# Opening of a fused matmul, GELU, matmul: four x tiles loaded and transposed in halves of K, and the first products in another order

## The chip, the cores and the metric

The kernel runs on one core of a Trainium2 chip. The metric is the time of one execution on the device in microseconds (us); of several executions the median counts. The core has a matrix engine (TensorE, PE in the profile; its weight loads are PEld), a vector engine (VectorE, DVE), an activation engine (ScalarE, ACT), a general engine (GpSimd, POOL), and a queue engine (SyncE, SP). DMAs are issued from SP, ACT and POOL; those that POOL issues also convert float32 in memory to bfloat16 on the core.

## What is computed

```python
batch, m, k, h, n = 16, 512, 768, 3072, 768
y = np.matmul(x, w1) + b1                    # x (16, 512, 768), w1 (768, 3072)
y = 0.5 * y * (1.0 + erf(y / np.sqrt(2.0)))
return np.matmul(y, w2).astype(np.float32)   # w2 (3072, 768)
```

All tensors are float32. The 16 x 512 rows of x are one list of 8192 rows.

## The kernel before, in words

Rows are worked on in passes (`pairs`) of 768 rows, that is two halves of 384, or six tiles of 128 rows; ten such passes, and one of 512 rows. In a pass the kernel first makes `g = gelu(x w1 + b1)`, transposed, with the hidden dimension on the partitions, then `g w2`. Both products use block schemes with fewer multiplications (seven products P1 to P7 for the first, fifteen M0 to M14 for the second); sums and differences of blocks are formed on VectorE. The forms of w1 are stored to a scratch tensor in memory (`w1f`) and read again in later passes; those of w2 stay on the core.

The first pass can't begin like the others, as nothing is loaded. Its opening is written out by hand, and the order of the calls is the order on each engine:

- x tiles 0 and 1 come as float32 through SP (`xw`, lines 466 and 467) and are converted by VectorE and ScalarE; tiles 2 to 5 come through POOL with conversion (`load_x0`, line 451) into `xb0`.
- w1 comes in groups of 384 columns (`load_w1`, line 351), each with six slices of 128 rows of K (`KC` = 6, `KH` = 3). Group 0 is loaded slice by slice (slices 0 and 1 together), group 1 in two halves, the others whole. Groups 2 and 3 lie in the tile `xft`.
- `turn_x0` (line 456) transposes a tile on TensorE: six transposes of 128 x 128 into a PSUM bank (two banks, `turns`, in turn), then a copy on VectorE into `xt`. Half 0 of `xt` holds tiles 0 to 2, half 1 tiles 3 to 5.
- `busy(n)` (line 440) issues n matmuls of 512 columns on zeros, whose result nobody reads: fillers.
- `first(half, c0, c1, k0, k1)` (line 498) multiplies w1 slices k0 to k1 of group 0 with columns c0 to c1 of a half of `xt`, for three blocks of 128 hidden columns at once; after the last slice and column, the GELU follows on ScalarE (`gelu1`).
- The bias is loaded as 24 rows, transposed on TensorE (line 529) into a corner of the second transpose bank, and copied to `b1t` by ScalarE.

Then `plain` (line 424) multiplies w1 groups 1, 2 and 3 with all of `xt`; `sum_x` and `form_w1` form sums on VectorE (copies for some w1 forms on ScalarE); and `step0` begins the seven-product scheme with block 3 (`product1`, line 148): P1 goes into a PSUM bank, ScalarE copies it to a second one (`c11`), and P2 adds into that.

Two things set the order around the change. Each engine takes its instructions in program order, and each waits for semaphores of those it depends on. And loads issued on POOL use eight semaphores in turn, so POOL issues a load only when the eighth one before it has landed.

## Time and profile before

| What | us |
|---|---|
| median of three runs | 873.79 (873.76 to 875.26) |
| profiled execution, its time | 873.71 |
| its span, first to last instruction | 871.9 |
| TensorE busy in the span | 866.8 (99%) |
| VectorE busy | 598.3 (69%) |
| ScalarE busy | 400.5 (46%) |
| first product (`first`) begins | 7.41 |
| first `plain` product begins | 15.34 |
| DMA bytes moved | 145.94 MB, mean 167 GB/s |

Times in the profile count from the start of the span. A line of a timeline has start, length, engine, source line, operation, output and inputs, shape and count; in brackets stands the idle time of the engine before it and what ended that. A line of the chain has start, length, and engine, tile and line. Matmuls are pipelined: one of 128 columns lasts 0.22 us but the next starts 0.056 us later. The length of a group of matmuls so holds one tail of about 0.16 us.

### The profile page before, as it was taken

The numbers are of one execution on the slowest core, as the hardware profiler recorded it, in microseconds if no ns is written. First come the engines' busy times: TensorE is split into PE (matmuls) and PEld (weight loads), VectorE is DVE, ScalarE is ACT, GpSimd is POOL, SyncE is SP. The second block draws the span as 40 slices with busy tenths as digits, with TensorE's granted clock in tenths as the row PEclk, the third lists the DMA queues.
The fourth block names the chain that finished last, engine by engine and source line by source line (L and its number), as shares of the span: only waits on it lengthen the run. The fifth ranks groups of instructions, "written<-read, shape, count | busy, mean of one in ns | idle before, by whom it ended". The sixth has DMA issues, their size and how long they took to land.

```text
span 871.9 us, 14069 instructions
## 1 busy us (share of the span) xinstructions
PE 866.8 (99%) x5479; PEld 531.2 (61%) x5479; DVE 598.3 (69%) x1090; ACT 400.5 (46%) x798; POOL 87.4 (10%) x160
## 2 busy tenths in 40 slices
PE   9999999999999999999999999999999999999998
PEld 5666556666666666666666666666666666666775
DVE  5799869657765775676577657756765776577654
ACT  3741673167127514731671275147316712751560
POOL 6120111010110001000101100010001011000000
PEclk9999999999999999999999999999999999999999
DMA  9997588176627736671756277366717663761521
GB/s 193 207 239 223 200 317 167 60 230 202 149 70 243 198 89 177 200 180 61 231 197 152 80 234 206 80 179 199 177 63 229 200 151 79 235 195 55 191 87 73
DMA packets 88935, 145.94 MB, mean 167 GB/s; under 512 B 50828, under 2 KB 68388, under 8 KB 88868
## 3 DMA queue, kind: packets, MB, share of 16 engines
q1 hardware_dynamic: 64256, 93.60, 35.7%
q0 software_dynamic: 24432, 50.73, 24.1%
q8 instruction: 43, 0.70, 0.3%
q10 hardware_dynamic: 180, 0.70, 0.2%
q14 instruction: 24, 0.20, 0.1%
HBM read 121.81 MB, written 33.42 MB: 178 GB/s over the span
## 4 chain that ended last, share of the span: by engine, by line
PE 97%; DMA 2%; POOL 0%; ACT 0%; DVE 0%; issue 0%; DVEq 0%; ACTq 0%; POOLq 0%
PE ps L237 47%; PE ps L162 45%; PE ps L431 3%; PE ps L822 1%; DMA w1f<-ot 1%; DMA st<-in_x_dram 1%; PE ps L504 0%; POOL w1t L78 0%; ACT g L145 0%; ACT ot L103 0%; POOL st L78 0%; DVE ps L113 0%; ACT ps L103 0%; DVE ev L113 0%; PE ps L459 0%
## 5 line engine op out<-in xcount | busy, mean ns | idle before, releaser
L162 PEld LDWEIGHTS <-w1t 128*128 128x128 bf16 x2421 | 236.9, 98 | 144.7 <-issue 1.4
L237 PE MATMUL ps<-w2t,g 128*128 128x384 bf16 x1512 | 257.8, 326 | 0.0
L162 PE MATMUL ps<-xft,w1t 128*128 128x384 bf16 (+1 forms) x1368 | 255.3, 320 | 0.3 <-ACT ps L103 0.3
L145 ACT ACTIVATE g<-ps,b1t 128x384 bf16<-128x384 f32 (+1 forms) x404 | 218.6, 570 | 74.5 <-PE ps L162 58.7
L237 PEld LDWEIGHTS <-g 128*128 128x128 bf16 x1512 | 147.9, 98 | 97.3
L162 PE MATMUL ps<-xt,w1t 128*128 128x384 bf16 (+1 forms) x1035 | 200.8, 320 | 0.1
L110 DVE TENSOR_TENSOR ot<-ot,ps 128x384 f32<-128x384 f32 x231 | 125.5, 552 | 106.0 <-PE ps L237 51.4
L237 PE MATMUL ps<-w2t,st 128*128 128x384 bf16 x1008 | 170.7, 326 | 0.0
L103 ACT COPY ot<-ps 128x384 f32<-128x384 f32 x129 | 60.8, 478 | 225.1 <-PE ps L237 206.3
L237 PEld LDWEIGHTS <-st 128*128 128x128 bf16 x1008 | 98.6, 98 | 65.2
L103 ACT COPY ps<-ps 128x384 f32<-128x384 f32 (+1 forms) x124 | 56.3, 454 | 142.5 <-PE ps L162 142.5
L113 DVE TENSOR_TENSOR ev<-ps,ev 128x384 f32<-128x384 f32 (+1 forms) x120 | 65.4, 545 | 73.5 <-PE ps L162 73.3
L113 DVE TENSOR_TENSOR ps<-ps,ev 128x384 f32<-128x384 f32 (+1 forms) x120 | 66.3, 553 | 44.0 <-PE ps L162 41.8
L105 DVE COPY ev<-ps 128x384 f32<-128x384 f32 (+1 forms) x120 | 65.0, 542 | 21.8 <-PE ps L162 21.7
L145 ACT ACTIVATE g<-ev,b1t 128x384 bf16<-128x384 f32 (+1 forms) x120 | 72.7, 606 | 15.3 <-DVE ev L113 15.3
L113 DVE TENSOR_TENSOR st<-g 128x1024 bf16<-128x1024 bf16 x107 | 73.0, 683 | 0.9 <-ACT g L145 0.9
L78 POOL DMA_DIRECT2D out_dram<-ot x60 | 32.7, 546 | 340.9 <-DVE ot L110 337.6
L113 DVE TENSOR_TENSOR g<-g 128x1024 bf16<-128x1024 bf16 x84 | 57.5, 684 | 0.5
L78 POOL DMA_DIRECT2D xb<-in_x_dram x38 | 20.5, 543 | 310.8 <-DMA xt<-xb 309.1
L110 DVE TENSOR_TENSOR g<-g 128x1024 bf16<-128x1024 bf16 x42 | 29.0, 690 | 1.1
L110 DVE TENSOR_TENSOR st<-st,g 128x1024 bf16<-128x1024 bf16 x42 | 28.9, 688 | 0.7
L431 PE MATMUL ps<-xt,w1t 128*128 128x384 bf16 x132 | 22.4, 326 | 0.0
(87 smaller groups left out, 291.6 us busy)
## 6 DMA issues: line engine op xcount, KB each, us to landing
w1t<-w1f SPq DMA_DIRECT2D x113, 672.0 KB, 5.2
out_dram<-ot POOLq DMA_DIRECT2D x60, 384.0 KB, 2.6
xb<-in_x_dram POOLq DMA_DIRECT2D x38, 192.0 KB, 4.7
w2t<-in_w_dram POOLq DMA_DIRECT2D x8, 576.0 KB, 20.4
w1f<-ot POOLq DMA_DIRECT2D x6, 672.0 KB, 8.2
ot<-in_x_dram POOLq DMA_DIRECT2D x18, 192.0 KB, 7.2
w1t<-in_w_dram POOLq DMA_DIRECT2D x4, 576.0 KB, 20.1
w1f<-ev SPq DMA_DIRECT2D x2, 672.0 KB, 3.5
```

What stands on the lines that cost most here:

```text
L78: inorder(queue.dma_start(out=out, in_=in_))
L103: inorder(nc.scalar.copy(out=dst, in_=src))
L105: inorder(nc.vector.tensor_copy(out=dst, in_=src))
L110: inorder(nc.vector.tensor_tensor(out=dst, in0=a, in1=b, op=ALU.add))
L113: inorder(nc.vector.tensor_tensor(out=dst, in0=a, in1=b, op=ALU.subtract))
L145: inorder(nc.scalar.activation(out=g[:, place_h(hc), half, :w], in_=src, func=ACTF.Gelu, bias=b1t[:, hc:hc + 1], scale=sign))
L162: inorder(nc.tensor.matmul(out=ps[:, :w], lhsT=forms[:, kc, :], rhs=moving1(m, kc, w, xs), start=(kc == 0 and m in ("P1", "P7")), stop=(kc ...
L237: inorder(nc.tensor.matmul(out=ps[:, :NB], lhsT=lhs[:, c, :], rhs=w2t[:, c, WF[m], :], start=(m in OPENS and c == 0), stop=(c == QC - 1), ...
L431: inorder(nc.tensor.matmul(out=py[:, :HW], lhsT=lhs[:, kc, (j % 3) * P:(j % 3 + 1) * P], rhs=xt[:, kc, half, :], start=(kc == 0), stop=(kc ...
L822: inorder(nc.tensor.matmul(out=ps[:, :c1 - c0], lhsT=lhs[:, c, :], rhs=w2t[:, c, WF[f], c0:c1], start=(f == terms[0][0] and c == 0), stop= ...
```

## The change

All of it is in the opening. Line numbers shift by up to 16 behind it: `first` has its products at line 511 and `turn_x0` its transposes at line 463.

- Tiles 2 to 5 are loaded in two halves of K each (columns 0 to 383 and 384 to 767), eight loads instead of four. The first halves stand beside w1 slices 0 to 2, the second halves among and behind slices 3 to 5. Slices 3 and 4 come in one load instead of two.
- `turn_x0` transposes a range of K: three transposes and a copy of 384 columns a call for tiles 2 to 5. The two banks are used in turn by the order of the calls, not by the tile.
- The calls of `first` are cut and ordered anew, to follow the order of the loads.
- `busy` takes a width. Seven fillers of 512 columns stay; five of 128 follow them; two of 512 and two of 128 stand where five of 512 stood.
- The bias transpose moves from before tile 0 to between tiles 0 and 1, and the bias copy on ScalarE so behind the conversion of tile 1.

```diff
-    def busy(n):
+    def busy(n, w=4 * P):
         for _ in range(n):
-            inorder(nc.tensor.matmul(out=pw[:], lhsT=warm[:, 0:P], rhs=warm, start=True, stop=True))
+            inorder(nc.tensor.matmul(out=pw[:, :w], lhsT=warm[:, 0:P], rhs=warm[:, :w], start=True, stop=True))
...
-    def load_x0(n):
-        dma(nc.gpsimd, out=xb0[:, n, :], in_=xf[n * P:(n + 1) * P, :])
+    def load_x0(n, k0, k1):
+        dma(nc.gpsimd, out=xb0[:, n, k0 * P:k1 * P], in_=xf[n * P:(n + 1) * P, k0 * P:k1 * P])
 
     turns = (bank(), bank())
 
-    def turn_x0(n, engine):
-        pt = turns[n % 2][:, :KC * P // 2].bitcast(BF16).rearrange("p (kc c) -> p kc c", kc=KC)
-        for kc in range(KC):
+    turned = 0
+
+    def turn_x0(n, k0=0, k1=KC):
+        nonlocal turned
+        pt = turns[turned % 2][:, :KC * P // 2].bitcast(BF16).rearrange("p (kc c) -> p kc c", kc=KC)
+        turned += 1
+        for kc in range(k0, k1):
             inorder(nc.tensor.transpose(out=pt[:, kc, :], in_=xb0[:, n, kc * P:(kc + 1) * P], identity=ident))
         half, c0 = place(HW, n)
-        copy(engine, xt[:, :, half, c0:c0 + P], pt)
+        copy("dve", xt[:, k0:k1, half, c0:c0 + P], pt[:, k0:k1])
...
-    load_x0(2)
+    load_x0(2, 0, KH)
     load_w1(0, 0, 2)
...
-    load_x0(3)
+    load_x0(3, 0, KH)
     load_w1(0, 2, 3)
-    load_w1(0, 3, 4)
-    load_x0(4)
-    load_w1(0, 4, 5)
-    load_x0(5)
+    load_x0(4, 0, KH)
+    load_x0(5, 0, KH)
+    load_x0(2, KH, KC)
+    load_w1(0, 3, 5)
+    load_x0(3, KH, KC)
     load_w1(0, 5, 6)
+    load_x0(4, KH, KC)
+    load_x0(5, KH, KC)
     load_w1(1, 0, KH)
     load_w1(1, KH, KC)
...
     busy(7)
+    busy(5, P)
+    copy("dve", xb0[:, 0, :], xw[:, 0, :])
+    turn_x0(0)
+    copy("act", xb0[:, 1, :], xw[:, 1, :])
+    busy(1)
     tb = turns[1][:, 448:448 + HC]
     inorder(nc.tensor.transpose(out=tb, in_=b1s, identity=ident32[:HC, :HC]))
     copy("act", b1t[:, :HC], tb)
-    copy("dve", xb0[:, 0, :], xw[:, 0, :])
-    turn_x0(0, "dve")
-    copy("act", xb0[:, 1, :], xw[:, 1, :])
-    busy(2)
-    turn_x0(1, "dve")
     busy(1)
-    turn_x0(2, "dve")
-    busy(2)
+    turn_x0(1)
+    turn_x0(2, 0, KH)
+    busy(2, P)
     first(0, 0, 2 * P, 0, 2)
+    turn_x0(3, 0, KH)
     first(0, 2 * P, HW, 0, 2)
-    turn_x0(3, "dve")
-    first(0, 0, HW, 2, 3)
-    first(1, 0, P, 0, 3)
+    first(0, 0, 2 * P, 2, 3)
+    first(1, 0, P, 0, 1)
+    turn_x0(4, 0, KH)
+    first(1, 0, P, 1, 2)
+    first(0, 2 * P, HW, 2, 3)
+    turn_x0(5, 0, KH)
+    first(1, 0, P, 2, 3)
+    first(1, P, 2 * P, 0, 1)
+    turn_x0(2, KH, KC)
+    first(1, P, 2 * P, 1, 2)
+    first(1, 2 * P, HW, 0, 2)
+    first(1, P, HW, 2, 3)
     first(0, 0, HW, 3, 4)
-    first(1, 0, P, 3, 4)
-    turn_x0(4, "dve")
+    turn_x0(3, KH, KC)
     first(0, 0, HW, 4, 5)
-    first(1, 0, P, 4, 5)
-    first(1, P, 2 * P, 0, 3)
-    turn_x0(5, "dve")
-    first(1, P, 2 * P, 3, 5)
+    first(1, 0, P, 3, 5)
+    turn_x0(4, KH, KC)
     first(0, 0, HW, 5, 6)
+    turn_x0(5, KH, KC)
     first(1, 0, P, 5, 6)
-    first(1, P, 2 * P, 5, 6)
-    first(1, 2 * P, HW, 0, 6)
+    first(1, P, 2 * P, 3, 6)
+    first(1, 2 * P, HW, 3, 6)
```

## The prediction, made before the result was known

> **What bounds the kernel now.** I read the page from the top: span, busy times, then the chain of work that ended last.
>
> ```profile
> span 871.9 us, 14069 instructions
> PE 866.8 (99%) x5479; PEld 531.2 (61%) x5479; DVE 598.3 (69%) x1090; ACT 400.5 (46%) x798; POOL 87.4 (10%) x160
> ...
> PE 97%; DMA 2%; POOL 0%; ACT 0%; DVE 0%; issue 0%; DVEq 0%; ACTq 0%; POOLq 0%
> ```
>
> TensorE carries 97% of the chain. Work on another engine is worth only the holes that it leaves in PE, and the change touches only the first 15 us. So I read the same chain for the first 60 us.
>
> ```profile
> 5.43 5.66 DMA st<-in_x_dram
> 11.09 0.05 issue
> 11.14 0.51 PE ps L459 x6
> 11.65 0.03 issue
> 11.68 1.33 PE ps L504 x15
> 13.01 0.34 PE ps L459 x6
> 13.34 2.16 PE ps L504 x33
> 15.50 8.78 PE ps L431 x54
> ```
>
> Until 11.09 the chain hangs on a landing (x tile 4); from 11.68 on it is PE without a hole. Next the timeline of the opening, for its order and its prices.
>
> ```profile
> 1.19 3.17 PE L442 MATMUL ps<-st 128*128 128x512 bf16 x7 [1.19 <-DVE st L471]
> ...
> 5.19 0.83 ACT L103 CAST st<-ot 128x768 bf16<-128x768 f32 x1 [0.39 <-DMA ot<-in_x_dram]
> ...
> 6.08 0.51 PE L459 MATMUL ps<-st 128*128 128x128 bf16 x6 [0.28 <-ACT st L103]
> ...
> 6.70 1.03 DVE L105 COPY xt<-ps 128x768 bf16<-128x768 bf16 x2 [0.74 <-PE ps L459]
> ...
> 6.97 0.59 PE L442 MATMUL ps<-st 128*128 128x512 bf16 x2
> ...
> 7.41 1.15 PE L504 MATMUL ps<-xt,w1t 128*128 128x256 bf16 x12
> ...
> 15.34 6.01 PE L431 MATMUL ps<-xt,w1t 128*128 128x384 bf16 x36
> ```
>
> Products begin at 7.41, and the next stage (L431) starts at 15.34. Prices, from starts: 56 ns for a product or transpose of 128 columns (0.34 for six), 109 for 256 columns, 162.5 for 384 (36 in 5.85 plus a tail of 0.16). Last, ScalarE behind the opening, which will matter:
>
> ```profile
> 22.00 0.83 ACT L103 COPY w1t<-xft 128x768 bf16<-128x768 bf16 x1
> 22.74 0.58 ACT L145 ACTIVATE g<-ps,b1t 128x384 bf16<-128x384 f32 x1
> 23.21 0.82 ACT L103 COPY ev<-xft 128x768 bf16<-128x768 bf16 x1
> 23.93 1.05 ACT L145 ACTIVATE g<-ps,b1t 128x384 bf16<-128x384 f32 x2
> 24.87 0.49 ACT L103 COPY ps<-ps 128x384 f32<-128x384 f32 x1
> ```
>
> From 22.00 ACT works without a hole; it started there because w1 group 3 (in xft) landed at 21.90 (issue 10.43, 11.5 to landing).
>
> **The change, part by part.**
>
> *The holes in the products.* From 7.41 to 15.34 are 7.93 us. The 78 products before are 60 x 0.056 + 6 x 0.109 + 12 x 0.1625 = 5.96, the transposes of tiles 3 to 5 18 x 0.056 = 1.01. The rest, 0.96, is holes, all before 11.68: waits for x tiles, w1 pieces and one DVE copy. After, there are again 78 products: 57 x 0.056 + 12 x 0.109 + 9 x 0.1625 = 5.96. Behind the first product stand 21 transposes (the second half of tile 2 moves behind it): 1.18, so 0.17 more.
>
> *Are the halves there in time?* Landings are from the list of DMA issues, asked load by load: issue plus time to landing. One unit is 96 KB: a half tile or one w1 slice. Before, tile 2 landed at 6.06 and w1 slice 5, twelve units later, at 13.04: 0.58 a unit. The next 18 units, to 21.90, took 0.49 each. A half tile has the shape of a w1 slice (128 rows of 384): slices landed 0.50 to 0.54 apart where the stream ran freely, whole tiles 0.91 to 1.15. So six halves cost 3.0 to 3.2 against 3.01 for tiles 3 to 5. For four tiles that is 0 to +0.3; I take +0.1, since both rows hold the same bytes. The first half of tile 2 lands at about 5.6 (half a tile earlier). Counting units at 0.49 to 0.58, against when PE gets there: w1 slices 3 and 4 at 10.0 to 10.8 against 11.1; second half of tile 3 at 10.5 to 11.4 against 11.6; of tile 4 at 11.5 to 12.6 against 12.7; of tile 5 at 12.0 to 13.1 against 13.4; the earlier ones have 0.4 or more. All hold, the slow end barely.
>
> *POOL.* Four more x loads at 0.55 and one w1 load fewer (0.56). POOL may have eight loads out: at 8.66 before, it sat 0.34 until an x tile had landed. Now this wait comes three loads earlier, in front of the second half of tile 3. POOL gets there at about 7.0, and the load it waits for lands at 5.6; the following ones have 0.7 or more. Behind it queue the w1 groups: group 1 is issued near 9.25 instead of 7.52, but the queue ahead is full until about 12.6. Nothing, then; without that cover the 1.7 us would show at 15.
>
> *DVE.* Four copies of 768 columns become eight of 384, each about 0.36 (0.56 less the 0.20 that 384 columns take at their share). A half turn's data are usable 0.78 after its first transpose (0.33 transposing, 0.04, 0.36, 0.05). One place in the new order is shorter: between the transposes of tile 3's second half (0.17) and its products stands only 0.49 of other products; PE waits 0.12. DVE's next work, the x sums, starts near 13.9 as before (13.85).
>
> *The bias and the fillers.* The bias transpose moves behind tile 0. It writes into the same PSUM bank as tile 1's transposes, so these gain a wait for ACT's bias copy, which now stands behind the 0.83 cast ending at 6.02. Its 0.18 overlaps the cast's tail: 0 to 0.18, I take 0.14, as successive ACT rows start about 0.09 before the former ends. Behind that wait stand tile 1 and every product. Tile 1 starts at 6.22, its DVE copy 0.62 later (6.08 to 6.70 before) takes 0.56, and the first product starts at 7.45 instead of 7.41: 0.04 lost. The fillers that go (five of 512 become two of 512 and two of 128 from here on) gain nothing, since the copy sets the start; the five of 128 before tile 0 fill a wait for its cast.
>
> *Sum for the opening:* 0.96 - 0.17 - 0.12 - 0.04 = 0.63 earlier: L431 at 14.71. Its w1 halves landed at 14.50 and 16.00, needed at 14.71 and 16.17.
>
> *What is late next.* The ACT rows. Product P2 adds into a bank that ACT fills by the copy of 24.87 to 25.36, so it can't begin before 25.43, unless group 3 lands earlier; before, PE got there at 26.07. Cap: 0.64 less the delay of group 3. With my +0.1 the gain is 0.54. Behind it nothing caps again: the w2 chunks landed 1.3 or more before DVE took them (chunk 7: 56.06 against 57.40), and the PE hole of 0.48 at 114.84 hangs on a store that POOL issues after an activation, so it moves along.
>
> The profiled execution took 873.71 us around its span of 871.9; the median of the runs is 873.79, 0.08 above. 873.79 - 0.54 = **873.25**, 0.06% faster. A change under 0.2% (1.75 us) is about what this kernel's measurement can't tell from none.
>
> **The rivals.**
>
> *The halves run freer.* At 0.49 a unit from the start, group 3 lands up to 1 us earlier and the cap goes; without the bias wait the opening gives 0.77 to 0.9. 872.95. For it: 0.49 later in the same trace. Against: 0.58 in this very stretch.
>
> *No gain.* One DMA engine lagged: slice 3 landed 1.29 after slice 2, where 0.5 is usual. Such a lag on a second half stops PE for 0.3 to 0.6, since only 0.2 to 0.3 of cover is left at the slow end; or group 3 lands 0.4 late. 873.7, within 0.3.
>
> *Slower: the clock.* The first seven fillers start 0.427 apart, the later ones 0.215: PE begins at half rate, for at least 1.19 to 4.15, though the granted clock reads 1.00. Between 4.86 and the first product the fillers were five of 0.215 before; now 0.54 in all, with holes of about 0.5 and 0.6. If PE falls back for a stretch as long as that first one (2.96), products lose half of it, 1.48: 873.25 + 1.48 = 874.7. It decides from 1.1 us of half rate on; beyond 0.2% it needs 4.6. Against: before, PE stood still for 0.44 at 5.6 and kept its rate. The Trainium skill, TensorE: Matmul & The Clock Gate, Part 1, has PE fall to half rate after an idle window of about 3.4 us, and Part 4 says that transposes don't count as busy; by that the stretch from 4.9 to 7.45 would be mostly idle, yet shorter than a window. The trace agrees that the rate doubles after some 3 us of fillers; no row here shows a fall.
>
> **How the numbers follow.** Forecast (gain 0.35 to 0.75): 0.52. Freer: 0.15. No gain: 0.19. Clock: 0.11. The rest, 0.03, for what I have not seen. The predicted time is the first's. From 872.7 (the freer case with its 0.9 and some) to 874.4 (no gain with its 0.3, and the shorter falls of the clock) hold over 8 in 10. Faster by over 0.2% would take 1.75 us, more than all holes of the opening: 0.04. Slower by over 0.2% is the long end of the clock case and the unseen: 0.09. Within: 0.87.
>
> **What would show it.** Right: products from about 7.45; hardly a hole in PE up to L431 at 14.6 to 14.9; ACT's copy chain still hanging on group 3 near 22; the loads of half tiles landing about 0.5 apart. Wrong: tile 1's transposes at 6.08 (no bias wait); a PE wait for an x half over 0.2; products 112 ns apart; P2 waiting past 25.6; or new holes behind 26.

## The result, and the profile after

The changed kernel takes 875.41 us (median of 22 runs, 874.19 to 877.0) where the kernel before takes 873.89 (22 runs beside them, 873.44 to 876.27). The ratio is 1.0015 with a 95% interval of 1.0009 to 1.0022: 1.3 us slower by the ratio. That is less than the 0.2% that the prediction calls about the limit of what can be told from no change, but the interval lies wholly above 1. The time is outside the forecast range of 872.7 to 874.4, and on the other side of no change than the 873.25 that was forecast. The profiled execution took 876.22 us.

The head of its page:

```profile
span 874.4 us, 14080 instructions
PE 867.1 (99%) x5483; PEld 531.9 (61%) x5483; DVE 599.0 (68%) x1094; ACT 400.3 (46%) x798; POOL 89.1 (10%) x163
...
PE 93%; DMA 4%; issue 1%; POOL 0%; ACT 0%; DVE 0%; SPq 0%; DVEq 0%; POOLq 0%; ACTq 0%
```

TensorE works as long as before (867.1 against 866.8); the span is 2.5 us longer, and DMA now has 4% of the chain where it had 2%. The chain over the first 60 us says where; each line is start, length, and what:

```profile
3.30 0.29 POOL st L107
3.60 0.50 POOL st L78
4.10 4.69 DMA w1t<-in_w_dram
8.79 0.28 issue
9.08 0.54 POOL st L78
9.62 0.72 POOL w1t L78
10.34 7.38 DMA w1t<-in_w_dram
17.73 0.05 issue
17.77 7.49 PE ps L431 x45
```

Before, the chain waited for a tile until 11.09 and was TensorE alone from 11.68 on. Now it is POOL and its loads up to 17.77: POOL's identity, POOL's issues, the landing of w1 slice 2 (8.79), the load of tile 5's second half, which had waited for that slice's semaphore, and the second half of w1 group 1, landing at 17.73. The timeline of the opening (start, length, engine, line, operation, and in brackets the idle time before and its cause):

```profile
6.19 0.66 PE L463 MATMUL ps<-st 128*128 128x128 bf16 x9
...
7.41 0.81 PE L511 MATMUL ps<-xt,w1t 128*128 128x256 bf16 x6 [0.44 <-DVE xt L105]
...
8.84 0.50 PEld L511 LDWEIGHTS <-w1t 128*128 128x128 bf16 x6 [0.28 <-DMA w1t<-in_w_dram]
9.08 0.54 POOL L78 DMA_DIRECT2D st<-in_x_dram  x1 [0.33 <-DMA w1t<-in_w_dram]
...
11.97 0.66 PE L511 MATMUL ps<-xt,w1t 128*128 128x384 bf16 x3 [0.46 <-DMA w1t<-in_w_dram]
```

TensorE's own times, as far as they hang on no load, are right to a few hundredths: tile 1's transposes at 6.19 (forecast 6.22), the first product at 7.41 (7.45), and between starts a wait of 0.124 us for the copy of tile 3's second half (0.12). What came late are loads. Two-microsecond stretches of the two kernels show them; the last two numbers are the time of all DMA packets as a share of 16 engines (over 1 where packets overlap), and GB/s. Before:

```profile
6.00:8.00 2.00, 1.92 (x21) 1.51 (x22) 1.03 (x2) 0.02 (x1) 2.00 (x4) 1.00 1.21 194
8.00:10.00 2.00, 1.97 (x26) 1.44 (x24) 0.56 (x1) 0.00 (x0) 1.66 (x3) 1.00 1.16 171
10.00:12.00 2.00, 1.85 (x19) 1.08 (x17) 0.32 (x1) 0.00 (x0) 1.72 (x3) 1.00 1.19 190
```

After:

```profile
6.00:8.00 2.00, 1.55 (x18) 1.25 (x18) 0.90 (x3) 0.14 (x1) 2.00 (x4) 1.00 1.02 134
8.00:10.00 2.00, 1.89 (x30) 1.67 (x28) 0.64 (x2) 0.00 (x0) 1.67 (x4) 1.00 1.18 146
10.00:12.00 2.00, 1.54 (x26) 1.25 (x24) 0.79 (x3) 0.00 (x0) 1.96 (x3) 1.00 1.19 174
```

From 6 to 12 us the changed kernel moves 60, 25 and 16 GB/s less than the one before, each over 2 us: some 200 KB, or two units of 96 KB. The landings (us, last of the 16 DMA engines, read from the trace load by load; "r1" is the changed kernel profiled once more):

```
                              before   forecast     after    r1
w1 slice 2                      8.85                 8.80    8.30
w1 slices 3 and 4     10.14 / 11.63   10.0-10.8     11.92   11.13
tile 3, second half      (8.37 whole) 10.5-11.4     12.39   11.63
tile 4, second half     (11.09 whole) 11.5-12.6     13.40   12.65
tile 5, second half     (12.54 whole) 12.0-13.1     13.93   13.13
group 1, first half            14.50     14.50      15.37   14.99
group 1, second half           16.00     16.00      17.73   17.51
   (the other 15 engines)      15.67                16.82   16.58
group 3                        21.90     21.9-22.3  23.04   22.97
group 1 begins on TensorE      15.34     14.71      15.57   15.04
its 19th product               18.27     17.64      19.25   19.03
```

(The 17.64 is 14.71 and 18 products of 0.1625.) So TensorE reaches group 1 at 15.57 and 15.04, that is 0.23 us later and 0.30 us earlier than before, and then stands for 0.74 us (r1: 1.05) in front of the second half. There is a second loss of the first profile, 1.60 us at 84.2, where products of line 237 wait for ScalarE and this for a store; r1 doesn't have it. It is taken up below.

### The profile page after: what moved, and what is told of

It is laid out like the page before. It is cut to its first block, busy times and chain, and to the rows that moved or that the text cites. A ratio compares the mean times of both kernels' runs of the same rounds, so it can differ in the third digit from the quotient of the medians.

```text
span 874.4 us, 14080 instructions
## 1 busy us (share of the span) xinstructions
PE 867.1 (99%) x5483; PEld 531.9 (61%) x5483; DVE 599.0 (68%) x1094; ACT 400.3 (46%) x798; POOL 89.1 (10%) x163
## 4 chain that ended last, share of the span: by engine, by line
PE 93%; DMA 4%; issue 1%; POOL 0%; ACT 0%; DVE 0%; SPq 0%; DVEq 0%; POOLq 0%; ACTq 0%
PE ps L162 45%; PE ps L237 44%; PE ps L431 3%; DMA w1t<-in_w_dram 1%; DMA xb<-in_x_dram 1%; DMA w1f<-ot 1%; PE ps L838 1%; DMA w1f<-ev 1%; DMA xt<-xb 0%; ACT ot L103 0%; POOL st L78 0%; POOL w1t L78 0%; SPq L295 0%; DVE ps L113 0%; ACT ps L103 0%
```

## The experiments

The expectations weigh theories against each other. A: POOL's issuing paces the loads. B: half rows are slow on the DMA engines by their shape. F: TensorE's instruction fetch holds one DMA engine up. Two things make the eighteen runs readable. The first: in every profile, span = start of the 19th product of group 1 + 853.4 to 854.0 us + the hole near 84 us, if there is one. (One exception, run 11, has 854.8, and two longer holes that its section names.) So in a profile a version's opening is worth what it does to that 19th product. A profile is one execution, though, and the ratio comes from eleven or more: run 14's 19th product starts at 19.20 and run 10's at 19.85, while their ratios are 0.9999 and 1.0011. The second: a load's *lead*, the time from its issue on POOL to its first landing; it says how far POOL is ahead of the DMA engines.

### Runs 1 to 4: again, fewer issues, and a slow POOL

The changed kernel once more:

> The changed kernel once more, for a second profile. In its first profile first halves of x tiles landed (first DMA engine) 2.9 us after their issue, about 0.55 apart, which is what POOL needs to issue one; before, this lead was 3.6 to 4.7. Both theories expect the second half of x tile 5 to land again at 13.5 to 14.3 and the second halves of w1 group 1 after 16.5 (before: 16.00). What it tells is the hole of 1.60 us at 84.2 of that profile: if it belongs to the change, it comes again (1 to 2 us between 80 and 90, span near 874.4); if it is a matter of how DMAs happen to meet, it is gone and the span is near 872.8 to 873.2.

875.55 us, ratio 1.0015 (1.0006 to 1.0024). Its profile has no hole at 84 us, but 0.23 us in front of group 1 and 1.05 us inside it.

Tiles 4 and 5 in one load, both for the first halves and for the second:

```diff
-    load_x0(4, 0, KH)
-    load_x0(5, 0, KH)
+    load_two(4, 0, KH)        # out=xb0[:, 4:6, :KH * P], one DMA
```

> The changed kernel, but the first halves of tiles 4 and 5 come in one load, and their second halves too: the same bytes in the same order and in the same pieces of 768 bytes a row, with two issues on POOL fewer (about 0.75 for a pair against 1.07 for two). Theory A (POOL's issuing paces the stream): the second half of tile 5 lands 0.4 to 0.7 earlier, near 13.3, and the second half of w1 group 1 near 17; time 0.3 to 0.7 us below the changed kernel. Theory B (the half rows themselves are slow on the DMA engines): landings and time within 0.2 us of the changed kernel.

874.57, ratio 1.0009 (1.0000 to 1.0018). TensorE waits 0.88 us for the pair (landing 9.73), and 0.26 us inside group 1, whose second half lands at 17.23. The last x half landed at 13.51, between the 13.93 and 13.13 of the changed kernel's two profiles, so this run decides little between A and B.

Pairs throughout, and slices 3 to 5 in one load:

```diff
-    load_x0(2, 0, KH)
+    load_two(2, 0, KH)
     load_w1(0, 0, 2)
...
-    load_x0(3, 0, KH)
     load_w1(0, 2, 3)
-    (eight loads)
+    load_two(4, 0, KH); load_two(2, KH, KC); load_w1(0, 3, 6); load_two(4, KH, KC)
```

> All half tiles in pairs (2 with 3, 4 with 5) and w1 slices 3 to 5 in one load: eight POOL issues in the opening instead of twelve, order of the products unchanged. The bytes up to the last x half are the same, in pieces of the same size. Theory A: the stream runs at about 0.5 us for 96 KB as in the steady part, the last x half lands at 12.3 to 12.8, the second half of w1 group 1 at 15.3 to 16; no PE wait for it, L431 at 14.7 to 15.1, time 0.3 to 0.8 us below the kernel before. Theory B: last x half at 13.5 or later, time at or above the kernel before.

874.74, ratio 1.0007 (0.9998 to 1.0015). Here the stream of the kernel before is back with the halves in it: last x half 13.24, group 1 at 14.66 and 16.12, group 3 at 21.96. The time isn't, since the large loads let TensorE wait 0.68 us at 7.9 and 0.66 us at 12.3. Theory A had the last half at 12.3 to 12.8 and the time under the kernel before; neither came. (The loads up to the last x half are seven, not the eight of the expectation.)

The kernel before, with six fills of about 0.25 us each on POOL between its loads:

```diff
     load_x0(3)
+    idle_pool()               # a POOL memset of 256 columns
     load_w1(0, 2, 3)
+    idle_pool()               # and so on behind each of the next four loads
```

> The kernel before, with six short fills of an unused patch on POOL (256 float32 a partition, an estimate of 0.35 us each from the 0.23 that the fill of 128 takes) between its loads of x tiles and w1 slices, about 2 us of POOL in all, which brings its issues to the pace of the changed kernel's; whole tiles, order and products as before. Theory A: the stream thins out as in the changed kernel, w1 slice 5 lands at 13.6 to 14.3 instead of 13.04, the second half of w1 group 1 after 16.5; time 0.4 to 1.2 us above the kernel before. Theory B: landings within 0.3 us of the kernel before, time within 0.3 us.

874.86, ratio 1.0008 (0.9998 to 1.0018). Slice 5 is issued at 8.31 instead of 7.00 and lands at 13.11 (13.04 before), as theory B had it; then the stream falls off, as theory A had it:

```profile
10.00:12.00 2.00, 2.00 (x26) 1.51 (x23) 0.56 (x1) 0.00 (x0) 2.00 (x4) 1.00 1.10 164
12.00:14.00 2.00, 2.00 (x30) 1.65 (x28) 0.79 (x2) 0.23 (x1) 2.00 (x4) 1.00 1.17 141
14.00:16.00 2.00, 1.83 (x27) 1.47 (x25) 1.93 (x4) 2.00 (x5) 1.41 (x3) 1.00 1.15 162
```

141 GB/s where the kernel before has 201, with whole tiles and only POOL made late; group 1's halves land 0.97 and 0.96 us later. So in this profile a late POOL alone makes such a dip. The time of the eleven runs isn't clear of no change. That the time of this profile (873.70) isn't longer comes from holes that it doesn't have elsewhere (0.28 us at 114.8 instead of 0.48).

### Runs 5 to 8: the identity's place, the instruction fetch, the fillers

Tile 3's first half ahead of the identity (one line moved):

> The changed kernel with one load moved: the first half of tile 3 is issued on POOL ahead of the identity (after w1 slices 0 and 1), where the changed kernel issues it behind. Four units of 96 KB instead of three are then queued while POOL builds the identity (2.6 to 3.5 us in the changed kernel, some 0.66 us later here). Theory A (the landings are late because POOL's queue runs dry while the identity is built and refills at POOL's pace of some 0.55 us a load): the dip of the changed kernel's bytes at 6 to 9 us (127, 140, 157 KB in a us) fills by about one unit; tile 3's first half lands near 7.1 to 7.3, w1 slice 2 and all that follow 0.3 to 0.6 us earlier than in the changed kernel's look of this chip, and half of it comes back at the end: 0.3 to 0.6 us under the changed kernel (875.0 to 875.3). Theory B (half rows are carried at 0.65 us a unit whatever the order): slice 2 and the second halves land as before within 0.15 us, and so does the time (875.6). A loss of up to 0.2 us would come from tile 0, whose transposes need the identity at 4.8 us, if it is late.

874.87, ratio 1.0012 (1.0001 to 1.0022). The stretch from 6 to 7 us fills (181 KB against 127), but slice 2 and its followers, issued at the same times as before, land hardly earlier, or later (slice 2 at 9.03 against 8.79 and 8.30, last half at 13.57 against 13.93 and 13.13): one unit of lead is soon used up. In its profile one DMA engine fell 2.6 us behind the fifteen others at group 1's first half (15.60 and 18.17), and TensorE stood still for 2.9 us. As a reading of its own this is neither theory's.

Nine of the sixteen fillers left out:

```diff
     busy(7)
-    busy(5, P)
...
-    busy(1)                   # twice, around the bias
...
-    busy(2, P)
```

> The changed kernel without nine of its sixteen fillers: the five of 128 columns ahead of tile 0, the two of 512 around the bias, the two of 128 ahead of the products. TensorE fetches its second 16 KB of instructions at its matmul 132 to 134 in every look so far; with nine matmuls fewer ahead, that is nine matmuls of 163 ns later in the products of group 1: 1.46 us later, at about 17.0 us where it was 15.7 and 15.5. Theory F (the fetch, 0.95 us on one DMA engine, is what makes the second half of group 1 land at 17.5 to 17.7): its last engine lands at 16.6 to 16.9, beside the next to last, and the hole of 0.74 to 1.05 us at 17.6 falls to under 0.2: 0.6 to 0.9 us under the changed kernel, 874.7 to 875.0. Rival (that engine is late for another reason): the landing and the hole stay, and the time with them. The fillers' other purpose, the clock: if tile 0's transposes or the first products run at half rate for want of them, the products start up to 0.4 us later than 7.41, and the gain is smaller by that.

876.44, ratio 1.0023 (1.0013 to 1.0034), 0.08% over the changed kernel by the ratios, whose intervals overlap, and not the gain that theory F had. Its profile can't tell the fetch: one engine brought x tile 1 at 7.24 instead of 5.00, TensorE idled from 5.2 to 8.2, and then worked at half rate. The columns of these stretches are length, then busy time of five engines, then the granted clock, the DMA share and GB/s:

```profile
8.00:9.00 1.00, 0.78 (x8) 0.86 (x9) 0.00 (x0) 0.17 (x2) 0.79 (x3) 0.50 1.30 184
9.00:11.00 2.00, 1.60 (x11) 1.04 (x9) 0.82 (x2) 0.00 (x0) 2.00 (x5) 0.50 1.23 179
11.00:13.00 2.00, 2.00 (x17) 1.80 (x16) 0.36 (x1) 0.00 (x0) 2.00 (x3) 0.50 1.21 154
```

The granted clock of 0.50 from 7.86 to 14.69 is the fall that the prediction's third rival was about: with the fillers it occurred in no profile, without nine of them in this one. The fetch came at 20.57, after group 1, whose second half all 16 engines landed between 15.85 and 17.71, the last two 0.26 us apart.

The kernel before with two of its first seven fillers cut into eight of 128 columns (six matmuls more, for an earlier fetch):

> The kernel before, with the last two of its first seven fillers cut into eight of 128 columns: the same columns and the same time on TensorE, six matmuls more. The fetch of the second 16 KB comes six matmuls earlier, at about 15.2 us instead of 16.16, while the second half of group 1 is still on its way (it landed at 16.00). Theory F (the fetch holds one DMA engine for 0.95 us): one engine of the second half lands at 16.8 to 17.0, the others by 16.0, and since TensorE needs it at 16.80, a hole of 0 to 0.3 us: 0 to 0.3 us over the kernel before. Rival (the fetch goes beside the loads at no cost): all engines by 16.0 to 16.1, the same time. Eight short matmuls may also issue at a wider pace than two long ones; that would show ahead of 4.3 us, where TensorE waits for tile 0 anyway, and cost nothing.

874.08, ratio 0.9999 (0.9990 to 1.0007). The fetch came at 15.76, not at 15.2, when group 1's second half had just landed (15.70). It so tests nothing; it shows that the narrow fillers cost nothing.

The nine issues of the next run, without the nine fillers:

> The changed kernel's products with nine issues in place of twelve, and without the nine fillers: tile 2's first half, w1 slices 0 and 1, tile 3's first half, then the identity, slice 2, tiles 4 and 5's first halves in one load, tiles 2 and 3's second halves in one, slices 3 and 4, slice 5, tiles 4 and 5's second halves in one. Theory A and F together: the landings return to 0.49 to 0.52 us a unit (tiles 4 and 5 by 9.2, slices 3 and 4 by 11.2, the last halves by 12.9, group 1's halves by 14.7 and 16.1), no hole over 0.2 us between 7.4 and 18 us, TensorE reaches group 1 at 14.7 to 14.9 instead of 15.34 in the kernel before, and the fetch at 16.2 does no harm. The whole is 0.3 to 0.6 us under the kernel before (873.4 to 873.7 where that is 874.0). Theory B (half rows are slow by their shape): holes of 0.5 to 0.9 us in front of the pair of tiles 4 and 5 and of slices 3 and 4 as in the second and third run, and 874.5 or more. Rival to both: the opening gains 0.5 us and later transfers, which meet each other otherwise, take it back: group 1 begins at 14.8 and the time is 874 or more.

875.28, ratio 1.0009 (1.0000 to 1.0018). Neither theory's number: the landings are not those hoped for (slices 3 and 4 at 12.24, last half 13.74), and TensorE kept to half rate until 9.97, products of 256 columns 213 ns apart instead of 109. The fetch came at 17.73, group 1's second half at 16.54 and 16.70 on the last two engines, without a lag.

### Runs 9 to 12: the parts alone

Nine issues in place of twelve, fillers as in the changed kernel:

```diff
     load_x0(2, 0, KH)
     load_w1(0, 0, 2)
+    load_x0(3, 0, KH)
     ...                       # identity
-    load_x0(3, 0, KH)
     load_w1(0, 2, 3)
-    (eight loads)
+    load_two(4, 0, KH); load_two(2, KH, KC); load_w1(0, 3, 5); load_w1(0, 5, 6); load_two(4, KH, KC)
```

> The loads of the eighth run (nine issues in place of twelve, tile 3's first half ahead of the identity) with all sixteen fillers of the changed kernel back, so that the clock is not in it. Theory A (POOL's pace makes the landings late): the last second halves of x by 13.2 instead of 13.9 and 13.1, no hole over 0.3 us up to group 1, which begins at 14.7 to 15.1; 0.5 us or more under the changed kernel (874.9 or less where the kernel before has 874.0). Theory F beside it: the fetch comes at TensorE's matmul 132, that is just as group 1 begins, 14.7 to 15.1, while its second half is on its way, so one DMA engine lands it 0.8 to 1 us behind the other fifteen and a hole of 0.4 to 0.9 us at 16.2 to 17 is left. Theory B (half rows are slow by their shape): landings as in the changed kernel, 875.5.

875.45, ratio 1.0012 (1.0003 to 1.0020). Theory A's landings didn't come (last half 14.57): the loads behind the identity have leads of 2.9, 3.5, 3.8, 4.2 and 4.0 us, hardly more than in the changed kernel, and three engines fell 1 to 2 us behind at the pair of tiles 4 and 5.

The same with eight matmuls fewer ahead of group 1:

> The ninth run's kernel with eight matmuls fewer ahead of group 1 and the clock's fillers kept nearly whole: the five fillers of 128 columns ahead of tile 0 become one of 512 and one of 128, the two ahead of the products go, and three pairs of products at the end of the opening are joined (tiles 4 and 5, slice 5). The fetch comes eight matmuls of 163 ns later, 1.3 us into group 1, at 16.0 to 16.4. Theory F: by then the second half of group 1 has landed, its sixteen engines within 0.5 us of each other as in the eighth run (16.54 to 16.70 between the last two), and the hole of the ninth run is gone: 0.4 to 0.9 us less than the ninth run, 874.0 to 874.4. Rival (the lagging engine has nothing to do with the fetch): the lag and the hole as in the ninth run, the same time.

875.13, ratio 1.0011 (1.0002 to 1.0020). The fetch came at 16.30 as meant, but group 1's second half was still under way (fifteen engines by 16.82), and the sixteenth landed it at 18.33. It was 0.05 us behind at the first half, so it lost 1.46 us there. The fetch isn't cleared by this, nor proved.

The halves alone: the kernel before, its order of loads and products, each tile of 2 to 5 as two loads.

```diff
-    load_x0(3)
+    load_x0(3, 0, KH)
+    load_x0(3, KH, KC)        # likewise tiles 2, 4 and 5
```

> One part of the change alone: the kernel before, its order of loads and products, with each of the tiles 2 to 5 loaded as two halves of K issued one behind the other; four issues more on POOL, thirteen in place of nine up to slice 5. Theory A: POOL issues slice 5 some 2.0 to 2.2 us later than 7.00, at 9.0 to 9.2, and the halves of group 1 at 9.6 and 10.8; with 2.9 us or more from issue to the first landing, slice 5 lands at 12.6 to 13.6, and group 1's halves at 14.9 to 15.4 and 16.4 to 17.3, 0.5 to 1.3 us later than before: 0.1 to 0.8 us over the kernel before. Theory B (by shape, 0.65 us for 96 KB in half rows): tile 5 lands 1 us later than 12.54 already. The prediction's view (issues and halves cost nothing but 0.1 us): the same time.

876.67, ratio 1.0028 (1.0018 to 1.0038): 2.4 us slower, more than the whole change, and more than theory A's 0.1 to 0.8. The landings are A's (slice 5 at 13.39, group 1's second half at 17.08) and not B's (tile 5 is there at 12.90, 0.36 us later than before, not 1). This profile's span is 1.5 us longer than before; the rest of the 2.4 isn't in it. The chain of the profile:

```profile
4.14 1.21 POOL st L78 x2
5.35 1.06 POOL w1t L78 x2
6.41 1.06 POOL st L78 x2
...
9.24 2.03 POOL w1t L78 x3
11.27 0.83 POOL xft L78
12.10 11.39 DMA xft<-in_w_dram
23.49 0.03 ACTq L103
...
26.55 0.39 ACT ps L103
26.94 0.04 issue
26.98 5.52 PE ps L162 x33
```

From 1.26 to 12.10 us the chain that ends last is POOL: its loads, one behind the other, and the identity (3.20 to 4.14); then group 3's landing at 23.49; then ScalarE's rows; then P2, 0.51 us late. That is the prediction's own cap, 1.5 us later than the 25.43 that it had. The leads from tile 3 to slice 5 are 2.6 to 3.0 us, all ten of them: they don't grow, so the DMA engines take the loads at the pace at which POOL writes them. (Its hole at 116.3 is 1.0 us instead of 0.48.)

The fillers and the bias transpose alone, on the kernel before:

> The other part alone: the kernel before, loads and products as they were, with the fillers and the bias transpose in the changed kernel's order (sixteen fillers in place of twelve, the bias behind tile 0, no filler between tiles 1 and 2). TensorE comes to tile 0 at the same time (4.7 to 4.9), to the products at 7.2 to 7.4; the fetch four matmuls earlier, at 15.5, where group 1's second half may land on one engine at 16.5 instead of 16.0, needed at 16.8: nothing. Both theories: within 0.2 us of the kernel before. If the small fillers raise the clock later (it rose at 5.2, 6.2 and 7.2 us in looks of the changed kernel and its kin, at 4.7 and 4.9 in those of the kernel before), tile 0 to 2's transposes take up to 0.7 us longer and the products start up to 0.3 us later; a hole in front of tile 4 shrinks by as much, so 0 to 0.2 us again.

874.06, ratio 1.0000 (0.9992 to 1.0009). This part is worth nothing either way. In its profile the clock rose at 6.97 us and the products began at 8.04, and still it has 872.5 of span.

### Runs 13 to 18: POOL relieved

The packets themselves tell more. A packet of these loads takes 79 ns (median); some take over 250. In the twenty profiles of this case, by the lead of the load that was under way (counted from one load's first landing to the next one's):

```
lead of the load, us     packets over 250 ns in a us
                         whole tiles    halves
under 3.2                     -          4.15
3.2 to 3.7                   2.76        3.19
3.7 to 4.2                   1.54        2.47
4.2 to 5.5                   2.31        2.77
over 5.5                     0.05        0.14
```

Long packets come where POOL is less than about 5.5 us ahead, and hardly any come where it is further ahead; between 3.2 and 5.5 us no slope is to be seen. Whole tiles have fewer in each row, but they also come in fewer and longer packets: between 3.2 and 5.5 us, 0.9 to 1.6 of 100 packets are long with whole tiles, and 1.1 to 1.4 with halves. The larger loads are also the later ones, with the longer leads; but among loads of one size the lead tells too. Group 1's halves (288 KB each) had 0 to 15 long packets, 4.9 in the mean, where their lead was under 5.5 us, and 0 or 1 above. (Whole tiles: the kernel before and runs 4, 7, 12, 15 and 18; halves: the others.) This table was made after the runs, from all of them; the next four were expected by an earlier state of it. They take work from POOL, and runs 13 to 15 do so without touching a load's shape: the zeros of the identity and its copy to bf16 move to VectorE.

```diff
-    make_identity(nc, ident32)                     # zeros and select on POOL
-    copy("pool", ident, ident32)
+    inorder(nc.vector.memset(ident32, 0.0))
+    make_identity(nc, ident32, nomemset=True)      # the select alone
+    copy("dve", ident, ident32)
```

The changed kernel with it:

> The changed kernel with the zeros of the identity written on VectorE and its copy to bf16 made there too; POOL keeps the one select of 0.29 us, so its loads behind it are issued some 0.45 us earlier (tile 3's first half at 3.1 instead of 3.55). Theory A', sharpened by the runs so far: a DMA engine stalls where POOL writes its work less than some 5 us ahead of it; packets over 250 ns came at 3.4 to 4.1 in a us where the first landing of a load was within 3.7 us of its issue, at 0.1 in a us above 5.5 us; the engine that lags in the opening stays late, and group 1's second half waits for it. So a lead longer by 0.45 us: fewer long packets (20 or fewer up to 14 us, against 31 and 25), tiles and slices 0.2 to 0.5 us earlier, group 1's second half at 16.8 to 17.3 instead of 17.5 and 17.7; 0.3 to 0.6 us under the changed kernel (874.9 to 875.2). Theory B (the halves' shape): no difference from the changed kernel, 875.5.

875.48 where the kernel before had 874.97 on that chip; ratio 1.0007 (0.9999 to 1.0016), half of the changed kernel's loss, though the two intervals overlap. POOL's loads come 0.56 us earlier, 19 packets are long up to 14 us (31 in the changed kernel, 25 in run 1), and up to the last half (12.49) all land 0.50 apart, as the prediction had it. Then group 1's engines spread (15.07 to 17.00). The profile has the hole at 84 us (1.89 us), so its span is no better than the changed kernel's; its 19th product starts at 18.53 instead of 19.25 and 19.03.

The nine issues with it:

> The ninth run's nine issues with the light identity. POOL is then as far ahead of the landings as in the third run (leads of 3.3, 3.9, 4.3, 4.6 and more behind the identity, against 2.9, 3.5, 3.8 and 4.2 in the ninth). Theory A': the stream of the third run (last halves 13.2, group 1's halves 14.7 and 16.1 to 16.4, group 3 at 22.0 to 22.3) without its two holes of 0.65 us: 0.3 to 1.0 us under the ninth run, 874.4 to 874.9. Theory B: 875.4 as the ninth.

874.79, ratio 0.9999 (0.9990 to 1.0008), against 1.0012 (1.0003 to 1.0020) without. Leads of 3.6, 4.3, 4.4 and 4.9 us behind the identity. One engine still brought group 1's second half late (16.21, 17.68), the fetch at 15.56 before it.

The control, the kernel before with it:

> Control: the kernel before with the light identity. Its leads behind the identity are 3.6 to 4.3 us, and 15 to 18 long packets are left in its opening; longer leads by 0.4 us can take some of them away, and its holes of 0.96 us between 9 and 12 us shrink by 0.1 to 0.4 us. Theory A': 0 to 0.3 us under the kernel before. Theory B: the same time as the kernel before within 0.1 us.

874.16, ratio 0.9996 (0.9987 to 1.0005). Leads 4.3 to 5.3; group 1 begins at 14.84 instead of 15.34.

And eight issues with it, slices 0 and 1 first:

```diff
-    load_x0(2, 0, KH)
     load_w1(0, 0, 2)
+    load_two(2, 0, KH)
     ...                       # the light identity
     load_w1(0, 2, 3)
+    load_two(4, 0, KH); load_two(2, KH, KC); load_w1(0, 3, 5); load_w1(0, 5, 6); load_two(4, KH, KC)
...
-    turn_x0(2, 0, KH)
     busy(2, P)
     first(0, 0, 2 * P, 0, 2)
+    turn_x0(2, 0, KH)
     turn_x0(3, 0, KH)
```

> Slices 0 and 1 first, then tiles 2 and 3's first halves in one load, the light identity, slice 2, tiles 4 and 5's first halves, tiles 2 and 3's second halves, slices 3 and 4, slice 5, tiles 4 and 5's second halves: eight issues; tiles 2 and 3 are transposed behind the first products, the rest of TensorE's order as in the changed kernel. Theory A': leads of 3.8 us at slice 2 and over 4.5 us from tile 2 and 3's second halves on, under 20 long packets, group 1's halves at 14.6 and 16.1, group 1 begins at 14.8 to 15.2, no hole over 0.4 us up to 18 us; 873.4 to 874.2, at or under the kernel before. Theory B: holes and 875 or more. If the opening's earlier end is not worth anything at the end: 874.0 to 874.4 with group 1 at 14.8.

874.05, ratio 0.9994 (0.9985 to 1.0002): clear of the changed kernel's 1.0009 to 1.0022, with the halves and its order of products nearly kept. Run 13, on the same chip, took 875.48. Once more, and the control once more:

> The sixteenth run's kernel once more, on whatever chip it meets: 0.9994 (0.9985 to 1.0002) of the kernel before then. Every profile so far has a span of 853.4 to 853.9 us plus the time at which the 19th product of group 1 starts, plus the hole in front of line 237 near 84 us where there is one. If the shorter queue is what counts, the 19th product starts at 17.9 to 18.6 us here (18.10 in the sixteenth run, 19.2 and 19.0 in the changed kernel), the span is 871.3 to 872.3 without such a hole, and the time 0 to 0.8 us under the kernel before. If the sixteenth run was chance: 0.5 us or more over it, as the changed kernel.

873.85, ratio 1.0000 (0.9991 to 1.0008). The opening of run 17 in the chain:

```profile
7.85 0.82 PE ps L512 x6
8.67 0.34 PE ps L467 x6
9.00 0.94 PE ps L512 x12
9.95 0.17 PE ps L467 x3
...
14.37 1.17 PE ps L512 x21
15.54 8.78 PE ps L431 x54
```

From the first product on nothing but TensorE, halves and all: the picture that the prediction had of the changed kernel. The forecast gain isn't there even so. The first product starts at 7.85, 0.40 us later than forecast, and with all of tile 2's transposes behind it (0.17 us more) group 1 starts where it did before. (The chain gives group 1 from the end of the piece ahead of it; its first start is 15.38.) The leads are 4.2 us at slice 2 and 4.9 in the mean, and 7 packets are long.

> The fifteenth run's kernel once more (0.9996, 0.9987 to 1.0005, then): 19th product of group 1 at 17.7 to 18.3, span 871.2 to 872.1 without a hole near 84 us, 0 to 0.8 us under the kernel before, and no worse than the seventeenth run's by 0.3 us. If the light identity wins nothing in the kernel before: the same time as before within 0.2 us.

874.21, ratio 0.9998 (0.9989 to 1.0007), with the hole near 84 us (1.41 us) in its profile.

All versions, in order of the mean lead of the loads behind the identity, up to the last of group 0 and x (whose landing is the third column of numbers):

```
                               loads  lead  last x  group 1,   19th      ratio to the
                                          or slice  2nd half   product   kernel before
r11 before, halves               13   2.9   13.39    17.08     18.61     1.0028
r6  changed, fewer fillers       12   3.1   13.67    17.71     22.27     1.0023
    changed                      12   3.2   13.93    17.73     19.25     1.0015
r5  changed, 3a ahead            12   3.3   13.57    19.20     21.15     1.0012
r1  changed, again               12   3.4   13.13    17.51     19.03     1.0015
r4  before, slow POOL             9   3.5   13.11    16.96     18.48     1.0008
r13 changed, light identity      12   3.5   12.49    17.00     18.53     1.0007
r2  tiles 4, 5 in pairs          10   3.7   13.51    17.23     18.75     1.0009
r9  nine issues                   9   3.9   14.57    17.49     19.68     1.0012
r10 nine, later fetch             9   3.9   13.90    18.33     19.85     1.0011
r8  nine, fewer fillers           9   4.0   13.74    16.70     18.90     1.0009
    before                        9   4.2   13.04    16.00     18.27     1
r12 before, new fillers           9   4.2   13.45    16.37     18.64     1.0000
r7  before, narrow fillers        9   4.3   12.78    15.70     17.96     0.9999
r3  pairs throughout              7   4.5   13.24    16.12     18.79     1.0007
r14 nine, light identity          9   4.5   13.41    17.68     19.20     0.9999
r15 before, light identity        9   4.8   12.21    15.34     17.77     0.9996
r18 the same again                9   4.8   12.78    15.70     17.93     0.9998
r16 eight, light identity         8   4.9   12.96    15.86     18.10     0.9994
r17 the same again                8   4.9   12.30    15.22     18.30     1.0000
```

By these ratios every version under 4.1 us of lead is slower than the kernel before, by 0.0007 to 0.0028 (the intervals of runs 4 and 13 contain 1, those of runs 2 and 8 begin at it), and with the exception of run 3 (large loads, TensorE waiting for them) none from 4.2 on is. Halves stand on both sides of that line. Whole tiles do too, but under it only with run 4, which isn't clear of 1. So it is POOL's lead that goes with the loss, and the halves' shape that doesn't. None of the versions is measurably faster than the kernel before; those with 4.8 and 4.9 us are its equals.

## Why the prediction was wrong, point by point

*TensorE's sum:* right. 0.17 for the moved half tile (three transposes at 0.056), 0.12 for the copy of tile 3 (0.124), 0.04 for the bias (under 0.01), a first product at 7.45 (7.41). From the first product to group 1 the sum has 7.26 us (7.45 to 14.71); r1 took 7.24 (7.57 to 15.04, less 0.23 of waiting for group 1). In run 17, where the loads are there, no hole among the products is over 0.12 us.

*The failed step, "POOL ... Nothing":* the step said that the queue ahead of POOL is full until about 12.6, and so four x loads more, with one w1 load fewer, cost nothing. The queue was not full. POOL's timeline before:

```profile
2.65 0.23 POOL masks.py:197 MEMSET st<- 128x128 f32 x1
...
3.56 0.55 POOL L78 DMA_DIRECT2D st<-in_x_dram  x1
4.11 1.34 POOL L78 DMA_DIRECT2D w1t<-in_w_dram  x2
5.43 0.55 POOL L78 DMA_DIRECT2D st<-in_x_dram  x1
```

And after:

```profile
2.64 0.23 POOL masks.py:197 MEMSET st<- 128x128 f32 x1
...
3.55 0.55 POOL L78 DMA_DIRECT2D st<-in_x_dram  x1
4.10 0.73 POOL L78 DMA_DIRECT2D w1t<-in_w_dram  x1
4.82 1.60 POOL L78 DMA_DIRECT2D st<-in_x_dram  x3
```

Issue, first landing and lead of the first five loads behind the identity, from the traces:

```
before                              after
tile 3         3.56   7.52  3.96    tile 3, 1st half  3.55  6.33  2.78
slice 2        4.11   8.03  3.92    slice 2           4.10  7.05  2.95
slice 3        4.91   8.52  3.61    tile 4, 1st half  4.82  7.70  2.88
tile 4         5.43   9.66  4.22    tile 5, 1st half  5.34  8.28  2.94
slice 4        5.96  10.19  4.24    tile 2, 2nd half  5.86  8.84  2.98
```

In the changed kernel POOL has issued three units of 96 KB when it turns to the identity (2.65 to 3.55), where the kernel before had issued four, and the first load behind it is one unit where it was two; from there on POOL writes one load in 0.52 to 0.75 us, and the first five land first 2.8 to 3.0 us after their issue begins, where the kernel before has 3.6 to 4.2. This gap and POOL's pace empty the queue, and between 6 and 8 us 134 GB/s are left of 194. From there on the DMA engines are slower even than POOL: from tile 3's first half to tile 5's second, first landings lie 0.70 us apart (6.33 to 12.60) where the issues lie 0.61 apart (3.55 to 9.08). The long packets of runs 13 to 18 fit this. Run 11, with the halves and nothing else, is 2.4 us slower and its chain is POOL from the first load to group 3; run 4 makes the same dip from whole tiles; runs 13 and 14 take 0.08% and 0.13% off by relieving POOL alone, beside the changed kernel and run 9 (the intervals overlap in both pairs); runs 16 and 17, with eight issues and POOL relieved, are clear of the changed kernel.

*"Landings at 0.49 to 0.58 a unit":* this followed from the step before. I took 0.58 for the slow end because it was this stretch's own rate, but it was the rate of nine issues; twelve issues at 0.55 with a gap of 0.9 didn't give it. The thirteen units from tile 2's first half (5.51) to tile 5's second (13.93) took 0.65 each, in r1 (5.42 to 13.13) 0.59. The +0.1 for the halves' shape, where the argument was spent, was right as nearly as can be seen: in run 13, with POOL 0.56 us earlier, the halves land 0.50 us apart.

*"Group 1 ... landed at 14.50 and 16.00, needed at 14.71 and 16.17":* I held these two times fixed. They moved to 15.37 and 17.73, and what remained of the margin of 0.2 us could take little: before the change, TensorE needed the halves 0.84 and 0.80 us after they had landed, and an engine a bit late was free. A change that brings TensorE forward spends this margin, so it has to be added to the costs of a late load, not only to the gain.

*The cap behind ScalarE:* the mechanism is real (run 11: P2 at 26.98, behind group 3's landing at 23.49), but in the changed kernel TensorE was so late that it never came to it.

*The rivals:* "No gain" had half of the mechanism, a lagging engine, but on a second half of an x tile, priced at 0.3 to 0.6 us, and ended at 873.7. It was one engine, at group 1's second half, for 0.9 us, on top of a stream that was late as a whole. I gave it 0.19, and took the late slice 3 of the profile before for one engine's chance, although its short lead stood there to be read (issue 4.91, first landing 8.52: 3.6 us). "Halves freer" (0.49 a unit from the start) is refuted for the changed kernel by its 0.65 and 0.59. "The clock": no fall in any profile with the fillers; run 6 shows one without them. The bias wait, the POOL semaphore wait (0.33 us at 9.08, in front of tile 5's second half, which the prediction had passed without one) were small.

*What stays open.* The forecast gain was seen in no version: where the loads were there in time (run 17), the first product came later. The nineteenth product is 0.77 (r1) to 0.98 us later than before; the medians lie 1.3 to 1.5 us apart. The rest isn't in r1's profile, whose time of 874.61 was the lowest of its eleven. The hole near 84 us, which five of the twenty profiles have (the changed kernel's, and runs 7, 13, 16 and 18: 0.77 to 1.89 us), is in both kinds of kernel, and r1 has none; that it comes more often when the stream is late was not shown. In the chain of the changed kernel it is this:

```profile
62.16 3.65 DMA xt<-xb
...
67.11 9.26 DMA xb<-in_x_dram
...
77.81 4.74 DMA w1f<-ev
...
84.22 10.56 PE ps L237 x64
```

A tile of the next pass took 9.26 us to land (the one in the kernel before: 6.5), a store waited behind it, and ScalarE behind the store. It seems to hang on how these transfers meet in one execution; no run tests that.

## What to carry to other kernels

Where loads need POOL to write them, count its issues as a stream of their own with a pace (here about 0.55 us for a tile, a half tile or one slice, 0.75 for two tiles or two slices) and a latency (2.6 to 3.0 us to the first landing where POOL set the pace), and work out for each load how far POOL is ahead of the DMA engines; cutting loads in two shortens that lead (run 11: 2.9 us in the mean, where it was 4.2). "The queue is full" has to be read from the time between a load's issue and its first landing, not from when the load ahead ends. And a consumer that is brought forward spends the margins of everything that lands just ahead of it: list these margins before the gain is booked.

## What was not expected

*A short lead costs more than the pace.* Where POOL is under some 5 us ahead, some packets take 250 to 1600 ns instead of 79, and single engines fell as much as 2.6 us behind the other fifteen (run 5). That the short lead makes these packets long is read from the table of runs 13 to 18; how it does so was not shown. The lateness stays: the last load of this stream, at 63 us, landed at 63.31 in the kernel before and 63.12 in run 17, at 64.95 in the changed kernel, and at 66.19 in run 5. The Trainium skill, DMA: Bandwidth & Descriptors (Anatomy of one DMA), gives such a transfer a fixed 2.0 us, most of it at the end, and calls the writing of descriptors small, with many to be had before a cost shows; by its formula 96 KB are an estimated 2.2 us. The traces of the changed kernel, where other loads were under way, have 2.8 to 3.0 us to the first landing of such a load, POOL's 0.55 us of issuing included, and 4.4 to the last, and thirteen loads for the bytes of nine cost 2.4 us (run 11); the measurement decides. The same page (Latency and other measured facts) has two engines usually slower and supposes contention at the descriptors; no run here shows which engine lagged.

*TensorE's instruction fetch.* One packet of 16,384 bytes on an instruction queue holds a DMA engine for 0.89 to 0.98 us; it came at about the 130th matmul (124th to 138th in the twenty profiles), between 15.1 and 20.6 us, about where group 1 begins. Where it fell 0.4 us or more before fifteen engines had group 1's second half (the changed kernel, runs 1, 2, 5, 10, 13, 14 and 16), the sixteenth came 0.3 to 2.1 us behind them; but in runs 5, 13 and 16 it had been as far behind at group 1's first half (2.57, 0.69 and 0.31 us). In the other five the gap grew by 0.6 to 1.5 us between the halves. Where the fetch fell later, the gap was 0.02 to 0.6 us (run 9's 0.8 is a lag from earlier), and in runs 15 and 17 the next load, group 2, has one engine 0.7 us behind, where nothing waits for it yet. That the fetch causes the gap is argued from this; the runs meant to show it (6, 7 and 10) did not.

*The clock's rise.* By the clock's records TensorE was granted full rate from 4.3 us on in the kernel before, from 5.3 and 5.6 in the changed one, and from between 4.0 and 10.0 in the others; the records of run 6 lie 3.41 and 6.83 us apart. The Trainium skill, TensorE: Matmul & The Clock Gate, Part 1, has a free-running window of 3413 ns that doesn't start with the kernel; the records agree with it. With the fillers the first product began between 7.2 and 8.1 us, mostly later where the clock rose later (7.41 with 5.3 us in the first profile, 7.57 with 5.6 in r1, 8.07 with 7.2 in run 5; but 7.41 with 6.0 in run 15).
